# Weight residuals by accumulating transfers, and Hyena transforms modulo 4 in float32, in a two-layer hybrid encoder

## The chip, the cores and the metric

The kernel runs on one core of one Trainium2 chip. The metric is the device time of one execution in microseconds (us), the median of several runs. TensorE multiplies matrices, VectorE, ScalarE and GpSimd do elementwise work, and SyncE issues transfers. The profile calls them PE (with PEld for its weight loads), DVE, ACT, POOL and SP.

## The reference

The model has two layers over 512 tokens of 1024 channels, all in float32:

```
h = RMSNorm(x);  p = h @ W_in                # 1024 x 2176
A: 384 channels, bidirectional RG-LRU with a convolution and a GeLU gate
B: 6 query heads, 2 key heads, attention within 128 tokens, with a sink logit
C: 256 channels, Hyena: y = irfft(rfft(z, 1024) * rfft(filter, 1024)) + z * bias, times a gate
x = x + concat(RMSNorm(A), RMSNorm(B), RMSNorm(C)) @ W_out      # 1024 x 1024
x = x + relu(RMSNorm(x) @ W_up)^2 @ W_down                      # 1024 x 4096, 4096 x 1024
```

After both layers comes one final RMSNorm.

## The kernel before, in words

**Products in three terms.** Float32 products are made from float32r operands. `split` and, for weights, `split_weight` round a value to a hi part (a cast) and keep the rest as a lo part (a subtraction). `mm3` issues three matmuls: hi by hi, hi by lo and lo by hi. So every weight tile of 128 by 1024 words (512 KB) costs a load, a cast on ACT or DVE, and a subtraction on DVE or POOL (`nc.any`).

**Weight tiles.** In both layers together there are 34 tiles of W_in (the first loaded in two halves), 16 of W_out, 64 of W_up, and 64 loads of W_down, which are combined into seven products for each of 16 quads (a Strassen-Winograd scheme, `PRODUCTS`), so 112 tiles. An in or an up tile feeds 24 matmuls of 512 columns. `weight` emits a tile `LA` tiles ahead of its use; `load` makes a tile's load wait for the end of an earlier tile's preparation. Raw words, hi parts and lo parts have pools of 6, 3 and 3 tiles.

**Order.** All instructions are first recorded and then ordered by `Plan.schedule`, a list scheduler with prices for each instruction. It decides at build time which engine takes an instruction that more than one could do. Work is given out in the order of recording, save where `plan.prio` is set. `SCRIPTS` sets the order of the steps in a layer's mixer: a number is an in tile, `G` the gates of the RG-LRU, `R` and `U` attention, `F` the Hyena filters, `I` the loading of what comes later, `H` the Hyena convolution, `S` and `A` the scans and the output of the RG-LRU, `N.` a group norm and `O.` an out projection. Where TensorE would sit idle, the planner puts in small bf16 matmuls whose results nobody reads (tile `wk`, in `filler`).

**Hyena.** The transform of length 1024 uses cosine and sine tables at odd frequencies. The sequence is split into even and odd positions (`dft`, called for `He`, `Ho`, `Xe`, `Xo`); the six tables, the filters, the inputs and the spectra `G` are each split into hi and lo, and each product is three matmuls of 256 columns. The inverse (tile `y`) does the same.

**End.** The last stage treats tokens in two halves. It scales `x` by the reciprocal norm, transposes it (tile `fin`), scales by the gain while leaving PSUM, and stores 16 pieces of 128 KB.

Of the kernel before, what the change touches and what calls it, by code (L numbers as in the profile page):

```python
# [10 lines left out]
F32 = mybir.dt.float32  # L11
# [19 lines left out]
    "8 10 F 1 9 3 0 G0 2 11 12 G2 G1 7 6 R 5 16 U U 15 U I 4 U S 13 U U 14 H U U NB A NA OA NC OB OC",  # L31
    "16 1 G1 6 2 0 15 G2 14 G0 11 13 12 7 H 9 8 10 R U 5 U 4 U U U U U 3 NC S U OC A NA OA NB OB",
)]
LA = 2
# [135 lines left out]
class Plan:  # L170
# [112 lines left out]
    def schedule(self):  # L283
# [31 lines left out]
        while pending:  # L315
            moved = True
            while moved:
                moved = False
                for e in engines:
# [76 lines left out]
                    if o.dma:  # L396
                        dma_free = max(dma_free, t + 1.0) + c
                        free_at[e] = t + 0.45
                        end = dma_free + 1.2
                    else:  # L400
                        end = t + c
                        free_at[e] = end
                    if LOCK and (e == "gpsimd" or e == "vector" and self.two_port(o)):
                        port_free = end
# [55 lines left out]
def encoder_kernel(ctx, tc, xT, w_in, w_out, w_up, w_down, gates, fw, par, trig, rope, decay, zemb, ident_d, maskb_d, yT):  # L460
# [81 lines left out]
    def split_weight(raw, n, c, hi, lo):  # L542
        plan.either(
            ("scalar", "copy", dict(out=hi[:, :n], in_=raw[:, :n])),
            ("vector", "tensor_copy", dict(out=hi[:, :n], in_=raw[:, :n])),
        )
        nc.any.tensor_tensor(out=lo[:, :n], in0=raw[:, :n], in1=hi[:, :n].bitcast(F32), op=ALU.subtract)
        return [(hi[:, q * c:q * c + c], lo[:, q * c:q * c + c]) for q in range(n // c)]

    def wtile(pool_, dt, name):  # L550
        return pool_.tile([128, 1024], dt, name=name, tag=name)

    def load(raw, src):
        if len(wdone) >= 3:
            plan.extra = {wdone[-3]}
# [32 lines left out]
    def emit_weight(key):  # L588
# [10 lines left out]
        else:  # L599
# [5 lines left out]
            out = split_weight(raw, 1024, 128 if kind in ("in", "up") else 512, wtile(whi, F32R, "wh"), wtile(wlo, F32R, "wl"))  # L605
# [128 lines left out]
    def load_trig(which):  # L734
        tr = {}
        for n in which:
            raw = Fs("traw")
            nc.sync.dma_start(out=raw, in_=trig[n])
            tr[n] = split(raw, "trig")
# [15 lines left out]
    def dft(tabs, src, out):  # L755

        th, tl = [t.rearrange("p (c k) -> p c k", c=2) for t in tabs]
        sh, sl = [t.rearrange("p (c k) -> p c k", c=2) for t in src]
        for kt in range(2):
            o = out[:, kt * 256:(kt + 1) * 256]  # L760
            for c in range(2):
                ks = slice(kt * 128, kt * 128 + 128)
                mm3(o, th[:, c, ks], tl[:, c, ks], sh[:, c, :], sl[:, c, :], c == 0, c == 1)

    def filters(i, tr):
# [15 lines left out]
        for par_ in range(2):  # L781
# [14 lines left out]
            hs.append(split(s, "hs"))  # L796
            hd.append(split(d, "hd"))
        H = {}
        for nm, tb, src in (("c", (0, 4), hs), ("s", (1, 5), hd)):
            pe = PMX("He")  # L800
            dft(tr[tb[0]], src[0], pe)
            e = Fs("e")
            nc.scalar.copy(out=e, in_=pe)
            po = PMX("Ho")
            dft(tr[tb[1]], src[1], po)
            for sg, op in (("+", ALU.add), ("-", ALU.subtract)):
                H[nm + sg] = Fs("H" + nm + ("p" if sg == "+" else "m"))
                nc.vector.tensor_tensor(out=H[nm + sg], in0=e, in1=po, op=op)
        return H

# [27 lines left out]
    nc.any.tensor_scalar(out=hbias, in0=pcols(_cols["ba"][0], _cols["bx"][1]), scalar1=0.5, scalar2=1.0, op0=ALU.mult, op1=ALU.mult)  # L838
    nc.any.tensor_scalar(out=nsink, in0=pcols(*_cols["sink"]), scalar1=-1.0, scalar2=1.0, op0=ALU.mult, op1=ALU.mult)
    nc.any.tensor_scalar(out=s_, in0=lam, scalar1=-1.0, scalar2=1.0, op0=ALU.mult, op1=ALU.mult)  # L840
    nc.vector.tensor_tensor(out=ex, in0=lam, in1=s_, op=ALU.min)
    act(ex, ex, AF.Exp)
    nc.any.tensor_scalar(out=s2, in0=ex, scalar1=2.0, scalar2=1.0, op0=ALU.add, op1=ALU.mult)
    nc.vector.reciprocal(out=s2, in_=s2)
    nc.any.tensor_tensor(out=s_, in0=ex, in1=s2, op=ALU.mult)
    nc.any.tensor_tensor(out=s2, in0=s_, in1=s_, op=ALU.mult)
    nc.any.memset(pl, 2.0 / 17.0)
    for q in range(7, -1, -1):
        nc.any.tensor_tensor(out=pl, in0=pl, in1=s2, op=ALU.mult)
        nc.any.tensor_scalar(out=pl, in0=pl, scalar1=2.0 / (2 * q + 1), scalar2=1.0, op0=ALU.add, op1=ALU.mult)  # L850
    nc.any.tensor_tensor(out=pl, in0=pl, in1=s_, op=ALU.mult)
    nc.vector.tensor_scalar(out=s_, in0=lam, scalar1=-1.0, scalar2=0.0, op0=ALU.mult, op1=ALU.max)
    nc.any.tensor_tensor(out=pl, in0=pl, in1=s_, op=ALU.add)
    nc.any.tensor_scalar(out=m4sp, in0=pl, scalar1=-4.0, scalar2=1.0, op0=ALU.mult, op1=ALU.mult)
    nc.any.tensor_scalar(out=p4sp, in0=pl, scalar1=4.0, scalar2=1.0, op0=ALU.mult, op1=ALU.mult)
# [8 lines left out]
    for i in range(DEPTH):  # L864
# [254 lines left out]
        def hyena(H, tr):  # L1119
# [5 lines left out]
            for par_ in range(2):  # L1125
                p = PMX("zt")
                for c in range(2):
                    for n in range(2):
                        src = v[n].rearrange("p (c s two) -> p c two s", c=2, two=2)[:, c, par_, :]
                        nc.tensor.transpose(p[:, c * 256 + n * 128:c * 256 + n * 128 + 128], src, ident)  # L1130
                zt.append(split(p, "zt"))
            X = {}
            for nm, tb in (("c", (0, 4)), ("s", (1, 5))):
                pe = PMX("Xe")
                dft(tr[tb[0]], zt[0], pe)
                e = Fs("e")
                nc.scalar.copy(out=e, in_=pe)
                po = PMX("Xo")
                dft(tr[tb[1]], zt[1], po)
                for sg, op in (("+", ALU.add), ("-", ALU.subtract)):  # L1140
                    X[nm + sg] = Fs("X")
                    nc.vector.tensor_tensor(out=X[nm + sg], in0=e, in1=po, op=op)
# [11 lines left out]
            for nm in "cs":  # L1154
                for pr, op in ((0, ALU.add), (1, ALU.subtract)):
                    g = Fs("G")
                    nc.any.tensor_tensor(out=g, in0=Y[nm + "+"], in1=Y[nm + "-"], op=op)
                    G[nm, pr] = split(g, "G")
            out = []
            for n in range(2):  # L1160
                p = PMX("y")
                for pr in range(2):
                    o = p[:, pr * 256:(pr + 1) * 256]
                    q = 0
                    for nm, tb in (("c", (2, 4)), ("s", (3, 5))):
                        th, tl = [t.rearrange("p (c k) -> p c k", c=2) for t in tr[tb[pr]]]
                        gh, gl = [t.rearrange("p (c k) -> p c k", c=2) for t in G[nm, pr]]
                        for c in range(2):
                            ch = slice(n * 128, n * 128 + 128)
                            mm3(o, gh[:, c, ch], gl[:, c, ch], th[:, c, :], tl[:, c, :], q == 0, q == 3)  # L1170
                            q += 1
# [5 lines left out]
                yv = y.rearrange("p (s two) -> p two s", two=2)  # L1177
                pv = p.rearrange("p (two s) -> p two s", two=2)
# [7 lines left out]
        for step in SCRIPTS[i]:  # L1186
            if step.isdigit():
                in_tile(int(step))
            elif step[0] == "G":
                lru_gates(int(step[1]))  # L1190
# [271 lines left out]
```

## Time and profile before

| | |
|---|---|
| median of 3 runs | 1106.83 us (1106.38 to 1107.84) |
| time of the profiled execution | 1107.12 us |
| its span (first to last instruction) | 1105.3 us |
| PE busy | 1090.6 us, 99% |
| DVE busy | 896.6 us, 81% |
| ACT busy | 588.6 us, 53% |
| POOL busy | 245.1 us, 22% |
| mean share of the transfer engines | 28.9% for the loads and stores |

Busy time of PE is the union of its instructions, and the ends of matmuls are modelled, so it doesn't tell how fast a matmul follows the one before. The start-to-start distance in the timeline, or the count in a stretch, does. Fillers count as busy.

### The profile page before, as it was taken

What the parts mean: (1) busy time and instruction counts of PE and PEld (TensorE: products, weight loads), DVE (VectorE), ACT (ScalarE), POOL (GpSimd) and SP (SyncE); (2) the same over time, 40 slices, a digit from 0 to 9 for tenths busy, and PEclk for the clock granted to TensorE, in tenths of its full rate; (3) what the DMA queues carried; (4) which work ended last, traced back from release to release, by engine and by line L of the source; (5) the groups of instructions that cost most, each with busy time, mean ns of one, the idle gap of its engine ahead of it and who ended that gap; (6) DMA issues with size and microseconds to landing.
All of it is one profiled execution on the core that took longest, in us unless ns stands there. A gap on an engine that the chain in (4) does not pass through costs nothing. (4 is left out here: it accounts for less than half of the span.)

```text
span 1105.3 us, 14023 instructions
## 1 busy us (share of the span) xinstructions
PE 1090.6 (99%) x5186; PEld 886.0 (80%) x5186; DVE 896.6 (81%) x1363; ACT 588.6 (53%) x957; POOL 245.1 (22%) x149
## 2 busy tenths in 40 slices
PE   9999999999999999999999999999999999999997
PEld 6778778888887788888887877788888888888886
DVE  8999988658779886797989999675597797788796
ACT  6677863455445454344366737745555445445444
POOL 0233443301011040110333234342011011011032
PEclk9999999999999999999999999999999999999999
DMA  9514101212243322422352221022141341342312
GB/s 341 189 52 156 67 32 54 100 59 94 77 146 103 109 90 83 134 76 77 104 173 78 79 74 58 20 74 92 64 130 46 129 134 59 114 133 70 102 58 77
DMA packets 35132, 107.90 MB, mean 98 GB/s; under 512 B 4150, under 2 KB 6710, under 8 KB 35064
## 3 DMA queue, kind: packets, MB, share of 16 engines
q1 hardware_dynamic: 35064, 107.01, 28.9%
q8 instruction: 41, 0.67, 0.3%
q14 instruction: 27, 0.22, 0.1%
HBM read 104.90 MB, written 2.10 MB: 97 GB/s over the span
## 5 line engine op out<-in xcount | busy, mean ns | idle before, releaser
L456 ACT CAST wh<-wr 128x1024 fp32r<-128x1024 f32 x197 | 207.4, 1054 | 346.4 <-PE pu L456 133.8
L456 DVE TENSOR_TENSOR wl<-wr,wh 128x1024 fp32r<-128x1024 f32 (+1 forms) x167 | 208.8, 1253 | 132.2 <-ACT wh L456 128.2
L456 PE MATMUL pu<-xgh,wh 128*128 128x512 f32 x512 | 199.4, 389 | 0.0
L456 PE MATMUL pu<-xgh,wl 128*128 128x512 f32 x512 | 199.4, 390 | 0.0
L456 PE MATMUL pu<-xgl,wh 128*128 128x512 f32 x512 | 199.3, 389 | 0.0
L456 POOL TENSOR_TENSOR wl<-wr,wh 128x1024 fp32r<-128x1024 f32 x60 | 146.2, 2439 | 228.2 <-ACT wh L456 174.7
L456 PEld LDWEIGHTS pu<-xgh,wl 128*128 128x128 f32 x512 | 96.1, 188 | 21.4 <-issue 1.6
L456 PEld LDWEIGHTS pu<-xgh,wh 128*128 128x128 f32 x512 | 96.1, 188 | 20.1 <-ACT xgh L456 0.2
L456 PEld LDWEIGHTS pu<-xgl,wh 128*128 128x128 f32 x512 | 96.1, 188 | 19.7
L456 PE MATMUL pin<-xgh,wh 128*128 128x512 f32 x272 | 107.7, 396 | 0.9 <-DVE p L456 0.4
L456 PE MATMUL pin<-xgh,wl 128*128 128x512 f32 x272 | 107.5, 395 | 0.0
L456 PE MATMUL pin<-xgl,wh 128*128 128x512 f32 x272 | 107.2, 394 | 0.3 <-DVE xgl L456 0.3
L456 POOL TENSOR_TENSOR s<-s,h 128x256 f32<-128x256 f32 x12 | 8.9, 742 | 397.4 <-ACT wh L456 388.5
L456 DVE TENSOR_TENSOR wr<-wr 128x1024 f32<-128x1024 f32 x61 | 72.8, 1219 | 0.0
L456 PEld LDWEIGHTS pin<-xgl,wh 128*128 128x128 f32 x272 | 51.1, 188 | 13.4 <-DVE xgl L456 2.1
L456 PEld LDWEIGHTS pin<-xgh,wh 128*128 128x128 f32 x272 | 51.1, 188 | 12.3 <-DVE p L456 0.8
L456 PEld LDWEIGHTS pin<-xgh,wl 128*128 128x128 f32 x272 | 51.2, 188 | 10.4 <-issue 0.2
L456 DVE SCALAR_TENSOR_TENSOR x<-po,tr,x 128x512 f32<-128x512 f32 x48 | 35.0, 747 | 23.2 <-PE po L456 19.8
L456 PE MATMUL po<-wh,ygh 128*128 128x512 f32 x128 | 50.6, 395 | 0.0
L456 PE MATMUL po<-wl,ygh 128*128 128x512 f32 x128 | 50.2, 392 | 0.0
L456 PE MATMUL po<-wh,ygl 128*128 128x512 f32 x128 | 50.0, 393 | 0.0
L456 DVE SCALAR_TENSOR_TENSOR x<-pY,r,x 128x512 f32<-128x512 f32 x64 | 45.6, 745 | 4.9 <-PE pY L456 4.9
(312 smaller groups left out, 2353.8 us busy)
## 6 DMA issues: line engine op xcount, KB each, us to landing
wr<-in_w_up SPq DMA_DIRECT2D x64, 512.0 KB, 3.4
wr<-in_w_down SPq DMA_DIRECT2D x64, 512.0 KB, 4.3
wr<-in_w_in SPq DMA_DIRECT2D x33, 512.0 KB, 4.0
wr<-in_w_out SPq DMA_DIRECT2D x16, 512.0 KB, 3.5
x<-in_xT SPq DMA_DIRECT2D x16, 256.0 KB, 5.6
dec<-in_decay SPq DMA_DIRECT2D x8, 256.0 KB, 7.3
out_y<-fin SPq DMA_DIRECT2D x16, 128.0 KB, 1.9
traw<-in_trig SPq DMA_DIRECT2D x6, 256.0 KB, 6.4
```

Source lines behind the costliest of these rows:

```text
L456: getattr(getattr(nc, o.eng), o.name)(*[res(a) for a in o.args], **{k: res(v) for k, v in o.kw.items()})
```

## The change

1. **Lo parts by transfers.** For in, out and up tiles from the fifth weight on, the lo tile is first written as the negated raw words rounded to float32r, on ACT or DVE; a transfer issued on POOL's queue then adds the raw words onto it. Down tiles and the first four weights keep the subtraction.
2. **One weight pool** of 13 tiles for raw, hi and lo parts, instead of 6, 3 and 3; the pool of 2 KB tiles shrinks from 69 to 67. The lookahead grows from 2 to 3 tiles, and a load waits for the preparation of the fourth tile back instead of the third. The planner's prices know transfers issued by POOL.
3. **Hyena modulo 4.** Positions are split by their remainder modulo 4. There are four tables, of 128 frequencies, used in float32 with no split; `sums` multiplies, `spectrum` combines by additions and subtractions, and the inverse has a further stage `U` of sums before its matmuls.
4. **Last stage** token tile by token tile, with a matmul against a diagonal matrix of the reciprocal norms in the place of scaling and transposing, and 8 stores of 256 KB in rows of 512 bytes.
5. **Order.** New `SCRIPTS`; the parameters of the gates are computed ahead of the first gates instead of at the very start.

```diff
-LA = 2
+LA = 3
+AHEAD = 4
+BY_DMA = ("in", "out", "up")
+WT, WRES = 13, 2
...
-    wraw = pool("wraw", 6, reserve=6)
-    whi = pool("whi", 3, reserve=3)
-    wlo = pool("wlo", 3, reserve=3)
-    sp = pool("sp", 69, reserve=RESERVE)
+    wraw = whi = wlo = pool("wt", WT, reserve=WRES)
+    sp = pool("sp", 67, reserve=RESERVE)
...
-    def split_weight(raw, n, c, hi, lo):
+    def split_weight(raw, n, c, hi, lo, by_dma=False):
...
-        nc.any.tensor_tensor(out=lo[:, :n], in0=raw[:, :n], in1=hi[:, :n].bitcast(F32), op=ALU.subtract)
+        if by_dma:
+
+            plan.either(
+                ("scalar", "activation", dict(out=lo[:, :n], in_=raw[:, :n], func=AF.Copy, scale=-1.0)),
+                ("vector", "tensor_scalar", dict(out=lo[:, :n], in0=raw[:, :n], scalar1=-1.0, scalar2=None, op0=ALU.mult)),
+            )
+            nc.gpsimd.dma_start(out=lo[:, :n].bitcast(F32), in_=raw[:, :n], accum_op=ALU.add)
+        else:
+            nc.any.tensor_tensor(out=lo[:, :n], in0=raw[:, :n], in1=hi[:, :n].bitcast(F32), op=ALU.subtract)
...
-        if len(wdone) >= 3:
-            plan.extra = {wdone[-3]}
+        if len(wdone) >= AHEAD:
+            plan.extra = {wdone[-AHEAD]}
...
+    def sums(tab, par, src, name):
+
+        p, b = PMX(name), Fs("b")
+        for c in range(2):
+            q, h = par + 2 * c, slice(c * 256, c * 256 + 256)
+            nc.tensor.matmul(out=p[:, h], lhsT=tab[:, q * 128:q * 128 + 128], rhs=src[:, h], start=True, stop=True)
+        nc.scalar.copy(out=b[:, :256], in_=p[:, 256:512])
+        return p[:, :256], b[:, :256]
+
+    def spectrum(tr, even, odd, name):
...
+        for nm, tab in (("c", 0), ("s", 1)):
+            a, b = sums(tr[tab], 0, even[tab], name + "e")
+            comb(e[nm][:, lo], a, b, ALU.add)
+            comb(e[nm][:, hi], *((a, b) if nm == "c" else (b, a)), ALU.subtract)
+        for nm, tab in (("c", 0), ("s", 1)):
+            for n in range(2 if odd[0] is not odd[1] else 1):
+                src = odd[tab] if n == 0 else odd[1 - tab]
+                a, b = sums(tr[tab], 1, src, name + "o")
...
+                for q in range(4):
+                    o = p[:, q * 128:q * 128 + 128]
+                    c = (q // 2) * 256 + n * 128
+                    for k, nm in enumerate("cs"):
+                        nc.tensor.matmul(out=o, lhsT=U[nm, q % 2][:, c:c + 128], rhs=tr[2 + k][:, q * 128:q * 128 + 128], start=k == 0, stop=k == 1)
...
+    for t in range(4):
         plan.prio = -0.5
...
+        r = token_rstd((t,))
+        d = Fs("diag")
+        nc.vector.tensor_scalar(out=d[:, :128], in0=ident, scalar1=r[:, 0:1], scalar2=1.0, op0=ALU.mult, op1=ALU.mult)
+        for n in range(2):
+            p, y = PMX("fin"), Fs("fin")
+            y.parts = True
+            for k in range(4):
+                c = slice(k * 128, k * 128 + 128)
+                nc.tensor.matmul(out=p[:, c], lhsT=x[t][n][:, c], rhs=d[:, :128], start=True, stop=True)
```

## Rows read from the trace of the kernel before

**Rows 1.** Page, part 1: busy time, share of the span and instructions.

```profile
PE 1090.6 (99%) x5186; PEld 886.0 (80%) x5186; DVE 896.6 (81%) x1363; ACT 588.6 (53%) x957; POOL 245.1 (22%) x149
```

**Rows 2.** Windows: busy us and instructions by engine, granted clock, transfers.

```profile
10.00:16.00 6.00, 6.00 (x29) 3.67 (x27) 6.00 (x16) 6.00 (x10) 0.00 (x0) 1.00 1.04 399
...
600.00:700.00 100.00, 96.78 (x518) 77.24 (x517) 96.12 (x159) 64.24 (x128) 35.73 (x23) 1.00 0.19 64
...
800.00:1085.00 285.00, 285.00 (x1262) 235.45 (x1261) 231.80 (x309) 136.01 (x181) 44.96 (x24) 1.00 0.29 95
```

**Rows 3.** Waits of PE: total us, times, longest.

```profile
PE vt L456 <- DVE p L456: 1.6, 1, 1.6
```

**Rows 4.** Windows of the filler's tile alone: PE busy us (instructions).

```profile
0.00:16.00 16.00, 7.12 (x42) 1.00 0.89 309
...
1090.00:1105.40 15.40, 3.72 (x31) 0.95 0.40 137
sum 1105.40, PE 21.48; mean PE 2.39
```

**Rows 5.** Groups by form on PE: the Hyena matmuls.

```profile
L456 PE MATMUL y<-trigh,Gh 128*128 128x256 f32 x32 | 8.9, 285 | 0.4 <-ACT Gh L456 0.4
...
L456 PE MATMUL Xo<-zth,trigh 128*128 128x256 f32 x16 | 4.6, 289 | 0.7 <-DVE rq L456 0.7
...
L456 PE MATMUL He<-hsl,trigh 128*128 128x256 f32 x8 | 2.3, 287 | 0.0
```

**Rows 6.** Timeline of PE: a run of Hyena matmuls, first and next after.

```profile
62.53 0.32 PE L456 MATMUL He<-hsl,trigh 128*128 128x256 f32 x1
...
68.20 0.40 PE L456 MATMUL pin<-xgh,wh 128*128 128x512 f32 x1
```

**Rows 7.** Timeline of PE: matmuls with float32 operands and what follows.

```profile
26.22 1.02 PE L456 MATMUL ssq<-sq,ones 128*128 128x512 f32 x2
27.17 1.07 PE L456 MATMUL f<-zemb,fw 33*64 33x512 f32 x2
...
54.97 3.70 PE L456 MATMUL f<-fw,h 64*128 64x512 f32 x8 [1.25 <-ACT h L456]
...
152.72 1.00 PE L456 MATMUL ssq<-ones,sq 128*128 128x1 f32 x8
153.58 0.38 PE L456 MATMUL wk<-warmc 128*128 128x256 bf16 x2
```

**Rows 8.** Groups by form: the preparation of weight tiles.

```profile
L456 DVE TENSOR_TENSOR wl<-wr,wh 128x1024 fp32r<-128x1024 f32 x165 | 207.4, 1260 | 132.2 <-ACT wh L456 128.2
...
L456 DVE CAST wh<-wr 128x1024 fp32r<-128x1024 f32 x28 | 19.2, 688 | 2.6 <-PE po L456 1.9 <-PE pu L456 0.7
...
L456 ACT CAST wh<-wr 128x1024 fp32r<-128x1024 f32 x197 | 207.4, 1054 | 346.4 <-PE pu L456 133.8 <-PE pY L456 82.0 <-PE pZ L456 45.0
...
L456 POOL TENSOR_TENSOR wl<-wr,wh 128x1024 fp32r<-128x1024 f32 x60 | 146.2, 2439 | 228.2 <-ACT wh L456 174.7 <-DVE wh L456 29.3 <-PE pin L456 14.0
```

**Rows 9.** Transfers: queue's packets, MB and share; issues, KB, us to landing.

```profile
q1 hardware_dynamic: 35064, 107.01, 28.9%
...
wr<-in_w_up SPq DMA_DIRECT2D x64, 512.0 KB, 3.4
wr<-in_w_down SPq DMA_DIRECT2D x64, 512.0 KB, 4.3
```

**Rows 10.** Timeline of the end, and the landing of the stores.

```profile
1091.40 0.75 DVE L456 SCALAR_TENSOR_TENSOR x<-pY,r,x 128x512 f32<-128x512 f32 x1 [0.34 <-PE pY L456]
...
1094.08 8.76 SPq L456 DMA_DIRECT2D out_y<-fin  x16
...
DMA to landing us min/median/max: 1.8/1.9/4.2
```

**Rows 11.** Timeline of DVE at the start.

```profile
12.51 0.17 DVE L456 TENSOR_SCALAR sp<-sp 128x12 f32<-128x12 f32 x1
12.58 0.74 DVE L456 SCALAR_TENSOR_TENSOR xgl<-x,pall,xgh 128x512 fp32r<-128x512 f32 x1
```

More of the change, by code (lines that the diff above doesn't have):

```diff
@@ L604, in emit_weight @@
                 load(raw, {"in": w_in, "up": w_up}[kind][i, key[2]] if kind != "out" else w_out[i, key[2]])
-            out = split_weight(raw, 1024, 128 if kind in ("in", "up") else 512, wtile(whi, F32R, "wh"), wtile(wlo, F32R, "wl"))
+            out = split_weight(raw, 1024, 128 if kind in ("in", "up") else 512, wtile(whi, F32R, "wh"), wtile(wlo, F32R, "wl"),
+                               kind in BY_DMA and wseq.index(key) >= 4)
         wdone.append(len(plan.ops) - 1)
@@ L736, in load_trig @@
         for n in which:
-            raw = Fs("traw")
-            nc.sync.dma_start(out=raw, in_=trig[n])
-            tr[n] = split(raw, "trig")
+            tr[n] = Fs("trig")
+            nc.sync.dma_start(out=tr[n], in_=trig[n])
         return tr
@@ L795, in filters @@
                 nc.any.tensor_tensor(out=d[:, cs], in0=f[:, 0:256], in1=f[:, 256:512], op=ALU.subtract)
[L796 to L809, printed above, removed]
+            hs.append(s)
+            hd.append(d)
+        return spectrum(tr, [hs[0], hd[0]], [hs[1], hd[1]], "H")
     def conv(i, u, taps, wname, bname, j, nj, centre):
@@ L837, in encoder_kernel @@
     hbias, nsink = ptile(12, "hbias"), ptile(6, "nsink")
[L838 to L850, printed above, removed]
@@ L1128, in hyena @@
                     for n in range(2):
-                        src = v[n].rearrange("p (c s two) -> p c two s", c=2, two=2)[:, c, par_, :]
+                        src = v[n].rearrange("p (r four) -> p four r", four=4)[:, par_ + 2 * c, :]
                         nc.tensor.transpose(p[:, c * 256 + n * 128:c * 256 + n * 128 + 128], src, ident)
[L1131 to L1142, printed above, removed]
+                z = Fs("zt")
+                rounded(z, p)
+                zt.append(z)
+            X = spectrum(tr, [zt[0], zt[0]], [zt[1], zt[1]], "X")
             Y = {}
@@ L1157, in hyena @@
                     nc.any.tensor_tensor(out=g, in0=Y[nm + "+"], in1=Y[nm + "-"], op=op)
-                    G[nm, pr] = split(g, "G")
+                    G[nm, pr] = g
+            U = {}
+            lo, hi = slice(0, 256), slice(256, 512)
+            for pr in range(2):
+                c, d = G["c", pr], G["s", pr]
+                U["c", pr], U["s", pr] = Fs("U"), Fs("U")
+                for nm, a, b in (("c", c, (c, d)[pr]), ("s", d, (d, c)[pr])):
+                    plus = nm == "c" or pr == 1
+                    nc.any.tensor_tensor(out=U[nm, pr][:, lo], in0=a[:, lo], in1=b[:, hi], op=ALU.add if plus else ALU.subtract)
+                    nc.any.tensor_tensor(out=U[nm, pr][:, hi], in0=a[:, lo], in1=b[:, hi], op=ALU.subtract if plus else ALU.add)
             out = []
@@ L1176, in hyena @@
                 )
-                yv = y.rearrange("p (s two) -> p two s", two=2)
-                pv = p.rearrange("p (two s) -> p two s", two=2)
+                yv = y.rearrange("p (r four) -> p four r", four=4)
+                pv = p.rearrange("p (four r) -> p four r", four=4)
                 nc.vector.scalar_tensor_tensor(out=yv, in0=pv, scalar=1.0 / 512.0, in1=yv, op0=ALU.mult, op1=ALU.add)
@@ L1189, in encoder_kernel @@
             elif step[0] == "G":
+                if i == 0 and not lru_st:
+                    gate_parameters()
                 lru_gates(int(step[1]))
```

109 lines of the change are left out of this document (55 added, 54 removed).

## The prediction

> **What bounds the kernel now.** I read the page's busy times first: PE is busy 99% of the span, DVE 81%, ACT 53%, POOL 22% [rows 1]. Since fillers count as busy, the second view is the windows. In the MLP of the second layer PE issues 1262 matmuls in 285 us, one every 0.226 us, and DVE is busy 232 of the 285 us [rows 2]. That is a pure PE bound: nothing but fewer or shorter matmuls makes this stretch shorter. From 600 to 700 us, the mixer of the second layer, DVE is busy 96% and PE's union falls to 96.8 us [rows 2]; there both engines are near their limit. At the start, from 10 to 16 us, DVE and ACT are busy all the time and the transfer engines' share is 1.04 [rows 2].
>
> Third come PE's waits: the longest of eleven is 1.6 us, for a value from DVE, and none is for a weight tile [rows 3]. The pauses long enough for fillers are in the windows of the filler's tile: of 21.5 us, 7.1 stand in the first 16 us and 3.7 in the last 15.4 [rows 4]. So there are three places to gain: the matmuls themselves, the start, and the end. Taking the subtractions of weights off DVE and POOL is worth little as long as no PE wait is for weights.
>
> **The Hyena matmuls.** Before there are 3 forms of `y` with 32, 6 of `X` with 16 and 12 of `H` with 8 matmuls: 96 + 96 + 96 = 288, all of 256 columns [rows 5]. A run of 47 of them goes from 62.53 to 68.20 us, so 0.1206 us each [rows 6], and all 288 take 34.7 us. After, by the diff, a layer has 6 calls of `sums` for the filters (even twice, odd four times, since the two sources differ) and 4 for the inputs, with 2 matmuls each: 20 of 256 columns. The inverse has 2 x 4 x 2 = 16 of 128 columns. Both layers: 40 and 32.
>
> These are float32 matmuls, and a float32 matmul leaves two records: the one sum over `ones` stands in the timeline as x2, 0.95 us from its start to the next matmul's, 0.475 us a record for 512 columns [rows 7]. The filters' matmuls give 3.70 / 8 = 0.46 [rows 7]. So there will be 80 records of 256 and 64 of 128 columns. No row has these widths in float32. In proportion to the columns they cost 0.228 and 0.114, together 18.2 + 7.3 = 25.5 us, a gain of 9.2; with 0.475 / 2 and 0.475 / 4 it is 26.6 and 8.1. That proportion is nearly right is seen in float32r: half the columns cost 0.1206 / 0.226 = 0.53 of the time. The upper end: with one column a record takes 0.86 / 8 = 0.1075 us [rows 7], and if that is a fixed part, a straight line through 0.1075 and 0.475 gives 0.291 and 0.199, in all 36.0 us, a loss of 1.3. I take 26.7 us, **a gain of 8 us**, since the 0.53 puts it near the proportional end; bounds +9.2 and -1.3. The gain counts in full where PE is the bound. The chain of combinations behind `sums`, and the new stage `U`, are hidden by the out products of the other groups and the rest of attention; without this cover each layer would show a few us of DVE work. DVE's own Hyena work hardly changes: in a layer ten subtractions for lo parts go, and 24 additions of half tiles come on top of the 8 of whole ones.
>
> **Lo parts by transfer.** 30 in, 16 out and 64 up tiles, 110 in all, lose a subtraction of 1.26 us on DVE or 2.44 on POOL and gain a negation, which I price like a cast: 1.05 on ACT or 0.69 on DVE [rows 8]. At most 110 x 1.26 = 139 us leave DVE. On PE's path this is worth nothing in the MLP, where PE waits for no weight. In the mixer, where DVE is near its limit, part of the short waits may go: **a gain of 2 us**, between 0 and 6 (eleven waits sum to about 8, all behind DVE, ACT or the start).
>
> The price is the transfer. No row shows one that adds, nor any issued from POOL; the only load queue is SP's [rows 9]. Below, it can cost what a load costs: 3.4 to 4.3 us to land [rows 9], and in engine time 28.9% of 1105 us for 107 MB, so 1.57 us for 0.524 MB. Above, with both operands read, twice that: 8.6 us and 3.1 us. The Trainium skill's page Collectives: The Full Stack (The bandwidth ceiling) says that an adding transfer costs double because it has two reads, not because of the addition; by that the upper figures would hold, and no run here shows it yet. Engine time is enough either way: a quad has 4 up and 4 down loads, and 4 additions at the upper price: 8 x 1.57 + 4 x 3.1 = 25 us, while PE works 4 x 24 + 7 x 12 = 180 matmuls, 40.7 us.
>
> Latency is covered too. With a lookahead of 3 tiles there are 3 x 24 x 0.226 = 16.3 us between one tile's turn and the preparation that must be ready. Load 4.3, cast 1.05, negation 1.05 and addition 8.6 make 15.0 us. So I cost the edit **at nothing**. What hides it is the lookahead; without it each tile would be late by the difference. Behind the POOL issue wait POOL's subtractions for down tiles (2.44 us each), whose own lookahead is 5. The wider shared pool lets this many tiles be open; should it not, loads start later, and the same cover shrinks.
>
> **Start.** Between the `xgl` subtractions DVE does one gate-parameter operation of 0.17 us each [rows 11]; moved away, and with two table loads fewer in the first rush and no table split, the first tiles may come **1 us** earlier. Bounds: 2, and minus 2, because the first additions join transfers whose share is already 1.04.
>
> **End.** Sixteen stores take SP 8.76 us, 0.55 each, the last issued at about 1102.8, while the last `x` is final at 1092.15 [rows 10]. After, 2 stores follow the last token tile in the place of 8: 6 x 0.55 = 3.3 us. ACT and DVE no longer scale `x`. Against this, rows of 512 bytes may land later, up to 4.2 instead of 1.9 us [rows 10], and the first two tiles' 32 records (at 0.114, 3.6 us), recorded at a priority ahead of the products, may stand before the last products. **A gain of 3 us**, between 0 and 5.
>
> **The sum:** 8 + 2 + 1 + 3 = 14 us. The profiled execution took 1107.1 us, 0.3 above the median of 1106.8, so the median becomes 1092.8; I say 1093.
>
> **Rivals.**
> 1. *Weights come late (slower).* The in tiles follow each other in both mixers. The period of a tile is its whole latency over three tiles of lookahead. It equals 5.43 us of PE work at 16.3 us, so at an addition of 16.3 - 6.4 = 9.9 us from POOL's turn to landing. Beyond it each us costs 0.33 us a tile; over all 94 in and up tiles 31 us, over the 30 in tiles alone 10. The gain of 14 is eaten at 0.45 us beyond if all suffer, at 1.4 if only the in tiles do. A chance for this comes from POOL's place in order: an addition can queue behind one or two subtractions of 2.44 us, and 8.6 + 2.44 passes 9.9 by 1.1. Both up and in tiles late by 1.14 give 1093 + 36 = 1129; in tiles alone 1104. Against it: at the lower price of 4.3 the cover has room for both subtractions.
> 2. *DVE holds up POOL's transfers (slower).* As a mechanism here: POOL can't make a transfer ready while a DVE cast runs, and each addition waits for one cast of 0.69 us [rows 8]. Alone that uses part of the cover; on top of rival 1 it makes 8.6 + 2.44 + 0.69 = 11.73, 1.83 beyond the cover, and 1093 + 57 = 1150. The Trainium skill's page SBUF — State Buffer (SBUF: two separate sides) states such a lock, between two-port copies on DVE and the descriptors of transfers issued from POOL. It gives 3.1 us for a transfer of 0.62 alone; by those 2.5 us more, the additions would land after 11.1 us, 1.2 beyond the cover, and the time would be 1131. The rule speaks against this change, and this trace has no transfer from POOL to show it.
> 3. *Savings turn into fillers (nearly no change to small gain).* If the mixers are bound by DVE from 600 to 700 us [rows 2] and in the first mixer likewise, shorter matmuls leave PE waiting, and only end and start remain: 1103. Against it: PE's listed waits are short, and DVE loses more work than it gains.
> 4. *More comes back.* DVE relief removes most of the waits and the start's fillers shrink by half (3.5 us): 8 + 6 + 3.5 + 5 = 22.5, so 1084.
>
> **How the numbers follow.** Forecast 0.60, rival 1 0.13, rival 2 0.05, rival 3 0.12, rival 4 0.10. The forecast's own range is 1087 to 1099 (its terms' bounds rarely fall together). With rival 4 below and rival 3 above, 0.82 lies between 1083 and 1104; less what the Hyena matmuls' upper price could push out, and with the mild part of rival 1 (in tiles alone, 1104 and some us), the range is 1083 to 1110. A change of 0.2%, 2.2 us, is about what a measurement of this kernel can tell from none. Faster: the forecast, rivals 3 and 4 without some mixed cases that end near no change, and a little of rival 1: 0.80. Same, from those mixed cases and the mildest of rival 1: 0.05. Slower, the rest of rivals 1 and 2: 0.15.
>
> **What would show it.** `He`, `Ho`, `Xe`, `Xo` with 256-column float32 records near 0.23 us apart, and 64 `y` records near 0.11; PE without waits for `wl`; additions landing under 9.9 us after POOL's turn; the last store issued within 8 us of the last `x`; DVE busy below 850 us. Wrong: PE waiting for DMA of `wl`, more fillers in the mixers, or 128-column records near 0.2.

## The result and the profile after

The change makes the kernel slower: 1115.08 us median of 18 runs against 1106.9 us of the kernel before in the same runs, ratio 1.0055 (95% interval 1.0042 to 1.0068). The forecast was 1093. The profiled execution took 1115.37 us, its span is 1113.5.

The page of the kernel after, part 1 and two queues of part 3 (packets, MB, share of 16 engines):

```profile
PE 1094.0 (98%) x5081; PEld 880.1 (79%) x5081; DVE 886.5 (80%) x1447; ACT 586.8 (53%) x957; POOL 211.3 (19%) x205
...
q0 software_dynamic: 15840, 57.68, 28.3%
q1 hardware_dynamic: 36696, 106.49, 26.7%
```

Against [rows 1] PE has 105 matmul records fewer, and DVE lost only 10 us, not the up to 139 that the 110 subtractions are worth. The windows of [rows 2]:

```profile
10.00:16.00 6.00, 5.91 (x27) 3.80 (x27) 6.00 (x10) 6.00 (x11) 0.00 (x0) 1.00 1.05 403
600.00:700.00 100.00, 96.94 (x508) 76.76 (x508) 91.22 (x171) 62.34 (x123) 21.93 (x22) 1.00 0.55 132
800.00:1085.00 285.00, 285.00 (x1271) 233.13 (x1270) 234.97 (x326) 124.38 (x165) 30.63 (x30) 1.00 0.51 142
```

The start is as before, the share of the transfer engines rises from 0.19 to 0.55 in the mixer and from 0.29 to 0.51 in the MLP, and DVE does as much in the MLP as before. There DVE has 51 subtractions instead of 62, but also all 24 negations of up tiles (16.6 us), while POOL's subtractions went from 16 to 2: the planner filled the freed time with work that ACT (136 to 124 us) and POOL (45 to 31) had. The windows of the filler's tile, cut by stage:

```profile
0.00:16.00 16.00, 7.21 (x41) 1.00 0.87 308
16.00:200.00 184.00, 0.49 (x3) 0.96 0.60 159
200.00:560.00 360.00, 4.53 (x32) 1.00 0.54 147
560.00:760.00 200.00, 5.67 (x40) 1.00 0.60 144
760.00:1090.00 330.00, 5.58 (x40) 1.00 0.52 142
```

From 16 to 200 us there are hardly any fillers, but the granted clock is 0.96. The waits of PE, to be held against [rows 3]:

```profile
PE pt L460 <- DVE e L460: 3.1, 1, 3.1
PE s L460 <- DVE kh L460: 2.0, 1, 2.0
PE fin L460 <- DVE ms L460: 1.4, 1, 1.4
```

The timeline of the kernel after, on several engines (start, us, operation, and in brackets the idle time ahead with its releaser). The new Hyena matmuls (`He`, `Ho`, `y`) are in it, and three places that cost time:

```profile
60.21 0.97 PE L460 MATMUL gate<-xch,gth 128*128 128x512 f32 x3 [1.24 <-ACT xch L460]
61.10 6.34 PE L460 MATMUL f<-fw,h 64*128 64x512 f32 x8
67.38 0.80 PE L460 MATMUL gate<-xcl,gth 128*128 128x512 f32 x1
...
72.93 1.02 PE L460 MATMUL He<-hd,trig 128*128 128x256 f32 x4
73.79 1.03 PE L460 MATMUL Ho<-hs,trig 128*128 128x256 f32 x4
74.65 1.89 PE L460 MATMUL Ho<-hd,trig 128*128 128x256 f32 x8
...
110.64 0.85 SPq L460 DMA_DIRECT2D trig<-in_trig  x2
111.54 7.14 SPq L460 DMA_DIRECT2D x<-in_xT  x8
119.74 7.24 SPq L460 DMA_DIRECT2D wr<-in_w_out  x3
128.96 0.69 DVE L460 CAST wh<-wr 128x1024 fp32r<-128x1024 f32 x1 [3.65 <-DMA wr<-in_w_out]
128.97 1.06 ACT L460 ACTIVATE wl<-wr 128x1024 fp32r<-128x1024 f32 x1 [3.10 <-DMA wr<-in_w_out]
129.97 0.45 PE L460 MATMUL pt<-ident,e 128*128 128x128 f32 x2 [3.11 <-DVE e L460]
...
193.21 2.84 PE L460 MATMUL y<-trig,U 128*128 128x128 f32 x24
195.81 0.48 PE L460 MATMUL po<-wh,ygh 128*128 128x512 f32 x1
...
938.98 1.22 DVE L460 TENSOR_TENSOR wl<-wr,wh 128x1024 fp32r<-128x1024 f32 x1
941.88 1.27 PE L460 MATMUL wk<-warmc 128*128 128x256 bf16 x10
942.25 0.75 DVE L460 SCALAR_TENSOR_TENSOR x<-pY,r,x 128x512 f32<-128x512 f32 x1
943.05 0.50 PE L460 MATMUL pY<-wh,sah 128*128 128x512 f32 x1
```

What to see there:

- *The matmuls.* Four records of `He` take 0.86 us, so 0.215 each; 24 of `y` take 2.60, 0.108 each. For 80 and 64 records that is 17.2 + 6.9 = 24 us in place of 34.7 [rows 5, 6].
- *The stall at 127 us.* In the attention of the first mixer PE waits for `e` on DVE. DVE stands at the cast of a W_out tile whose load SP issued at 119.74, behind the loads of tables and `x`, and which landed 9.1 us later; ACT stands at the negation of the same tile. Neither engine can pass it, so ready attention work waits for a weight whose own turn comes later.
- *The clock.* The eight `f` took 6.34 us, where before they took 3.70 [rows 7].
- *The MLP.* PE had nothing for 1.17 us at 941.88: the next product (P6, the fourth of the quad on PE here) goes into the bank `pY` that DVE's update of `x` at 942.25 frees, and DVE did four `wl` subtractions of 1.22 us, this one the last, from 933.69 on ahead of it.

The windows for the clock (the column after POOL is the granted clock):

```profile
60.00:70.00 10.00, 9.79 (x17) 4.78 (x18) 8.03 (x12) 4.31 (x7) 2.90 (x3) 0.60 0.39 92
70.00:80.00 10.00, 10.00 (x42) 8.30 (x42) 8.09 (x18) 8.22 (x17) 1.70 (x1) 0.89 0.14 27
...
130.00:140.00 10.00, 10.00 (x47) 7.16 (x48) 7.48 (x18) 7.71 (x16) 2.75 (x3) 0.83 0.28 57
```

At the lower level (1.2 GHz, 0.5) for (0.40 + 0.11 + 0.17) x 20 = 13.6 us, PE loses 6.8 us of work. The fall at 130 follows the stall of 3.1 us. The fall at 62 follows a wait of 1.24 us; but before, a wait of 1.25 us ahead of the same eight `f` brought none [rows 7]. In the trace of e8_end_alone (below), whose first mixer is written as in the kernel before, the clock did fall there: the eight `f` took 5.44 us after a wait of 1.23, at 0.80 from 50 to 60 us. So after this wait the clock falls in some executions and not in others, also at the old lookahead; what decides is open. The runs of this kernel lie between 1109.65 us (mean granted clock 0.998) and 1119.6 (0.993), those of the kernel before around 1107 us (0.999) or around 1111 (0.995).

Transfers (issues, KB, median us to landing), and the issue of the additions on POOL (ns, least, median, most):

```profile
wl<-wr POOLq DMA_DIRECT2D x110, 512.0 KB, 5.4
wr<-in_w_up SPq DMA_DIRECT2D x64, 512.0 KB, 4.5
wr<-in_w_down SPq DMA_DIRECT2D x64, 512.0 KB, 7.0
```

```profile
L460 POOL DMA_DIRECT2D wl<-wr x110: 850/862/1155, 20.4 to 1042.2; - x110
```

An addition lands after 5.4 us, between the bounds 4.3 and 8.6; the slowest of the 110 took 9.8. The loads land later than before [rows 9].

### The profile page after: what moved, and what is told of

Its sections match the earlier page's. It is cut to its first block, busy times and chain, and to the rows that moved or that the text cites. A ratio compares the mean times of both kernels' runs of the same rounds, so it can differ in the third digit from the quotient of the medians.

```text
span 1113.5 us, 14163 instructions
## 1 busy us (share of the span) xinstructions
PE 1094.0 (98%) x5081; PEld 880.1 (79%) x5081; DVE 886.5 (80%) x1447; ACT 586.8 (53%) x957; POOL 211.3 (19%) x205
## 3 DMA queue, kind: packets, MB, share of 16 engines
q0 software_dynamic: 15840, 57.68, 28.3%
q1 hardware_dynamic: 36696, 106.49, 26.7%
## 4 chain that ended last, share of the span: by engine, by line
PE 82%; DVE 8%; DMA 4%; ACT 3%; issue 2%; SPq 0%; POOL 0%; ACTq 0%; DVEq 0%; POOLq 0%
PE pu L460 31%; PE pY L460 16%; PE pZ L460 8%; PE pin L460 7%; PE po L460 7%; PE pX L460 4%; PE gate L460 1%; PE pv L460 1%; PE f L460 1%; PE pt L460 1%; DMA wr<-in_w_in 1%; DVE wl L460 1%; DVE tg L460 1%; DMA zemb<-in_zemb 1%; DMA wr<-in_w_out 1%
## 5 line engine op out<-in xcount | busy, mean ns | idle before, releaser
L460 ACT CAST wh<-wr 128x1024 fp32r<-128x1024 f32 x190 | 198.7, 1051 | 289.8 <-DMA wr<-in_w_up 88.8
L460 POOL DMA_DIRECT2D wl<-wr x110 | 96.3, 878 | 529.1 <-DVE wl L460 192.1
L460 DVE TENSOR_TENSOR wl<-wr,wh 128x1024 fp32r<-128x1024 f32 (+1 forms) x108 | 131.1, 1220 | 22.0 <-ACT wh L460 19.5
L460 PEld LDWEIGHTS pu<-xgh,wh 128*128 128x128 f32 x512 | 96.1, 188 | 20.9 <-issue 1.1
L460 DVE TENSOR_SCALAR wl<-wr 128x1024 fp32r<-128x1024 f32 x73 | 51.8, 710 | 28.4 <-DMA wr<-in_w_up 22.9
L460 ACT ACTIVATE relu<-pu 128x512 f32<-128x512 f32 x64 | 37.9, 592 | 39.9 <-PE pu L460 39.9
L460 DVE TENSOR_TENSOR s<-h 128x256 f32<-128x256 f32 x62 | 28.1, 454 | 34.5 <-ACT h L460 34.2
L460 DVE SCALAR_TENSOR_TENSOR x<-pZ,r,x 128x512 f32<-128x512 f32 x64 | 46.9, 747 | 8.5 <-PE pZ L460 8.4
```

Of the source, the lines that this page charges most:

```text
L460: getattr(getattr(nc, o.eng), o.name)(*[res(a) for a in o.args], **{k: res(v) for k, v in o.kw.items()})
```

## The experiments

Eighteen kernels ran. The table reads from each trace when PE starts the first up matmul (end of the first mixer), how long the first MLP, second mixer and second MLP take (to the last product of a layer, to the next layer's first up matmul, to the last product), all in us. Ratios are against the kernel before on the same chip; its median there was between 1107 and 1110, so kernels are compared by ratio. A row's stages are those of one execution, and time lost at the lower clock (half of what is spent at it) is in them: in mixer 1, 6.8 us of after, 5.1 of e6, f4 and g2, 3.4 of e7 and e8, 1.7 of e1, e2, f3, h4 and h6, none of the others; in mixer 2, 3.4 of e2 and h4, 1.7 of e8, f4, k1, k5 and l1.

| kernel | mixer 1 | MLP 1 | mixer 2 | MLP 2 | median | ratio (95%) |
|---|---|---|---|---|---|---|
| before | 218.0 | 344.2 | 201.4 | 327.4 | 1106.83 | |
| after | 221.1 | 343.8 | 200.4 | 332.9 | 1115.08 | 1.0055 (1.0042 to 1.0068) |
| e1_no_transfers | 227.0 | 345.1 | 203.3 | 331.9 | 1121.94 | 1.0118 (1.01 to 1.0136) |
| e2_no_transfers_old_pools | 224.4 | 339.1 | 207.4 | 327.4 | 1114.29 | 1.0046 (1.0029 to 1.0062) |
| e6_hyena_alone | 227.3 | 339.1 | 209.9 | 327.4 | 1116.02 | 1.0068 (1.0051 to 1.0084) |
| e8_end_alone | 220.4 | 344.1 | 202.7 | 327.4 | 1107.77 | 0.9997 (0.9985 to 1.001) |
| f1_before_one_product | 218.3 | 337.8 | 202.2 | 327.4 | 1101.01 | 0.9941 (0.9919 to 0.9964) |
| f4_hyena_without_U | 224.2 | 339.1 | 200.7 | 327.4 | 1104.36 | 0.9971 (0.9958 to 0.9984) |
| e7_update_first | 218.4 | 342.7 | 202.4 | 328.1 | 1109.18 | 1.0007 (0.9987 to 1.0027) |
| f3_inout_update_first | 217.4 | 340.9 | 197.5 | 327.5 | 1102.3 | 0.9954 (0.9935 to 0.9972) |
| h4_old_hyena | 225.7 | 339.9 | 206.2 | 329.0 | 1114.51 | 1.0052 (1.0033 to 1.0071) |
| h6_old_hyena_la2 | 223.6 | 339.4 | 201.8 | 329.0 | 1108.77 | 0.9997 (0.9983 to 1.001) |
| g5_la2 | 209.9 | 340.7 | 200.7 | 327.5 | 1096.13 | 0.9887 (0.9867 to 0.9908) |
| g2_in_only | 225.1 | 340.6 | 200.7 | 327.5 | 1109.97 | 1.0007 (0.9992 to 1.0023) |
| k2_la2 | 210.2 | 355.8 | 213.8 | 349.3 | 1146.26 | 1.0333 (1.0309 to 1.0358) |
| k1_no_update | 209.9 | 345.7 | 215.8 | 330.4 | 1118.3 | 1.0083 (1.0061 to 1.0105) |
| k5_up_too | 210.2 | 365.3 | 219.6 | 358.7 | 1170.46 | 1.0556 (1.0528 to 1.0584) |
| g3_before_update | 217.2 | 343.2 | 204.5 | 328.9 | 1110.49 | 1.0017 (1.0 to 1.0034) |
| l1_mixer_la2 | 210.6 | 343.8 | 215.3 | 333.6 | 1119.48 | 1.0096 (1.0073 to 1.0119) |
| l2_mixer_la2_update | 210.3 | 342.6 | 202.1 | 328.2 | 1100.0 | 0.9933 (0.9911 to 0.9955) |

**1. Transfers off, then pools and lookahead too, and the parts alone.** On the change:

```diff
e1:
-BY_DMA = ("in", "out", "up")
+BY_DMA = ()
e2, in addition:
-LA = 3
-AHEAD = 4
+LA = 2
+AHEAD = 3
-    wraw = whi = wlo = pool("wt", WT, reserve=WRES)
-    sp = pool("sp", 67, reserve=RESERVE)
+    wraw = pool("wraw", 6, reserve=6)
+    whi = pool("whi", 3, reserve=3)
+    wlo = pool("wlo", 3, reserve=3)
+    sp = pool("sp", 69, reserve=RESERVE)
```

> The changed kernel with all lo parts by subtraction again; shared pool, lookahead 3, Hyena modulo 4, last stage and order stay. Theory A (the adding transfers are the cost: they double the transfer work, loads land late, ACT and DVE stand in order behind a load, PE stops): the MLP of layer 2 goes back to a quad period of 40.8 us from 41.2 to 42.3, the clock stays near 1.0, time 1096 to 1101. Theory B (the shared pool and the longer lookahead bunch the preparation of down tiles ahead of the updates of x that PE waits for): the quads stay at 41.2 to 42.3, time 1104 to 1110. Theory C (the longer chain of the new Hyena and its place in the order starve PE in the mixers): mixers as in the changed kernel, 1108 or more.

> As the run without transfers, but also with the pools of 6, 3 and 3 tiles and the lookahead of 2 of before; Hyena modulo 4, last stage and new order stay. Theory A: within 2 us of the run without transfers, 1096 to 1101. Theory B: at least 5 us below it, about 1097 against 1104 to 1110. Theory C: still above 1105.

Without transfers the change is slower still, so they are not what costs. With the old pools and lookahead back, 7.6 us return: the MLPs are 10.5 us shorter, the mixers 1.5 longer together (e2 loses 3.4 us more there by the clock).

Then the kernel before with the new Hyena alone (`load_trig`, `sums` and `spectrum`, the stage `U`, the tables), and with the new last stage alone:

> The kernel before with the Hyena transforms modulo 4 alone, in the old order. Matmul work falls by 10 us by the records of the changed kernel (64 of 0.112 and 80 of 0.216 us against 288 of 0.1206). Theories A and B: 1097 to 1100. Theory C: 1105 or more, with PE waits in the mixers that were not there before.

> The kernel before with the new last stage alone. My forecast's term: 3 us shorter, 1104. The rival (the float32 matmuls of the first token tiles push the last products back by as much as the stores save): 1106 to 1108. In the changed kernel's trace the last product starts at 1098.2 and the span ends at 1113.5, 15.3 us, against 14.3 before, so this rival has the trace on its side.

The new Hyena alone costs 0.68%: each mixer grows by about 9 us (in mixer 1, 5.1 of them go with the clock). e2 has the new order and the new last stage besides, and comes to 1.0046: with no transfers, the order is worth 3 us at most in mixer 1 and, without the clock's part, some 6 in mixer 2. MLP 1 is 5 us shorter, but not by its filter matmuls. In the kernel before two quads had 2.04 us of fillers each ahead of P6, which are gone. The windows of the filler's tile by stage, the wait of PE, and its timeline at the inverse, in e6_hyena_alone:

```profile
16.00:234.00 218.00, 8.14 (x70) 0.98 0.28 99
234.00:573.00 339.00, 1.71 (x11) 1.00 0.31 105
573.00:784.00 211.00, 12.79 (x102) 1.00 0.19 65
```

```profile
PE y L456 <- DVE U L456: 2.5, 1, 2.5
```

```profile
183.71 5.52 PE L456 MATMUL wk<-warmc 128*128 128x256 bf16 x49
189.07 3.79 PE L456 MATMUL y<-trig,U 128*128 128x128 f32 x32
```

With the chain through `U`, PE has nothing ahead of `y`: the fillers of the mixers are 20.9 us, where the kernel before has 2.66 + 0.76. The chain is not all of it. DVE ends the eight `U` sums of mixer 1 at 185.7 us, 3.4 us before the first `y`, and the planner fixed the number of fillers at build time; what else held `y` is not shown. And the longest wait of PE in e6 is another, 3.9 us for `p` on DVE at 113 us, which f4 has too. The new last stage alone changes nothing.

**2. Is PE's time in the mixers worth anything?** In the kernel before, only hi by hi in the Hyena transforms; and e6_hyena_alone without `U`:

```diff
f1:
-                mm3(o, th[:, c, ks], tl[:, c, ks], sh[:, c, :], sl[:, c, :], c == 0, c == 1)
+                nc.tensor.matmul(out=o, lhsT=th[:, c, ks], rhs=sh[:, c, :], start=c == 0, stop=c == 1)
f4:
+            U = G
```

(The inverse in f1 likewise.)

> The kernel before, in whose Hyena transforms only the product of the hi parts is computed (192 of 288 matmuls left out, 23 us of TensorE time; all casts, subtractions and additions on the other engines stay). Theory M (in the mixers the elementwise work on DVE and its chains are the bound; PE time saved there turns into fillers and waits, and only what is saved in the MLP, where the filters of layer 2 run, is gained): about 4 us for the MLP and little more, 1101 to 1106, with holes in the mixers. Theory P (PE is the bound throughout, as the prediction had it, and the loss of the new Hyena has another cause): 1084 to 1088.

> The kernel before with Hyena modulo 4 alone, as in e6, but with the 16 additions of half tiles of the stage U left out in each layer's eight sums (G goes straight into the inverse matmuls; the matmuls are as many). Theory M: the wait of y for U in mixer 1 (5.4 us of fillers in e6) and in mixer 2 (2.6 us) shrink by the chain left out, about 3 us each, so 1109 to 1113 against 1116 of e6. Theory P: within 1 us of e6.

Where 23 us of matmuls are left out, both mixers stay as long as they were; 6.4 us of MLP 1 are the gain, 3.8 of them in the quad with the filter matmuls; the two long quads are gone here too. Leaving out the 16 half-tile additions (eight a layer) makes e6_hyena_alone 1.0% faster, some 11 us, more than the 3 to 7 expected, while eight of them took 2.77 us on DVE, so 5.5 for all. Without transfers the mixers end by chains, not by PE: the mechanism of rival 3.

**3. The order of the `x` update, and the up tiles.**

```diff
e7 (on the change):
+                    plan.prio = -1.5
                     nc.vector.scalar_tensor_tensor(out=x[k][n], in0=o, scalar=sc[:, k:k + 1], in1=x[k][n], op0=ALU.mult, op1=ALU.add)
+                    plan.prio = 0.0
f3, in addition:
-BY_DMA = ("in", "out", "up")
+BY_DMA = ("in", "out")
```

> The changed kernel with one priority altered: in the down products the update of x on DVE is recorded ahead of the preparation of weights. Theory B, kept for the MLP alone (the longer lookahead and the shared pool bunch four subtractions on DVE ahead of the update that frees the bank of the next product): the quads go from 41.2 to 42.3 back to 40.8 us, 4 to 6 us less in all at the same clock, 1109 to 1111. Rival (the weights themselves are late in the MLP): quads unchanged.

> As the run with the update first, and lo parts by transfers for in and out tiles alone; up tiles are subtracted again. If the transfers' worth lies in the mixers, where DVE is short of time, and their price in the MLP: quads at 40.8, mixers as in the changed kernel, 1106 to 1110. If the up tiles' transfers help too: 1112 or more.

With the update first every quad of the second MLP lasts 40.8 us again instead of 41.2 to 42.3: 4.8 us in MLP 2. Without the up tiles it gains 7 us more, 5 of them in mixer 2, where no up tile is used but which was planned anew; it is faster than the kernel before and below both expected ranges.

**4. Old Hyena beside the transfers, lookahead, in tiles alone.** h4 is f3 with the Hyena and `SCRIPTS` of before (and pools of 12 and 69, into which its tiles fit); h6 and g5 are h4 and f3 with `LA = 2` and `AHEAD = 3`; g2 is f3 with `BY_DMA = ("in",)`.

> The kernel before, plus the transfers for in and out tiles, plus the shared weight pool (12 tiles, 2 KB pool of 69), the lookahead of 3 tiles, the new last stage and the x update of the down products first: run f3_inout_update_first with the Hyena of before and the order of before. Theory M (the mixers end by DVE and its chains, and the new Hyena lengthens them though it shortens PE): the mixers come out below those of f3 (217 and 198 us), by 4 to 9 us each, MLP 1 longer by about 5 because the filters' matmuls are back, in all 1092 to 1101, faster than f3's 1102.3. Rival (with transfers the mixers are bound by PE, and the matmul saving is real there): the 10 us of matmuls come back, 1108 to 1113.

> Run h4_old_hyena with a lookahead of 2 tiles and a load waiting for the third preparation back, as before. Theory: two tiles of lookahead are 10.9 us, load 4.3, cast and negation 2.1 and addition 5.4 make 11.8, so each in tile would be late by about 1 us, and the mixers grow by 5 to 15 us in all against h4. Rival: the pool and not the lookahead decides when loads start, and the time is that of h4 within 3 us.

> Run f3_inout_update_first with a lookahead of 2 tiles and a load waiting for the third preparation back, as before. Theory (the late w_out load in mixer 1 stands in front of other casts, because it is asked for too early relative to its turn and behind loads of x and tables): with a shorter lookahead the cast is asked for later and the wait of 3.9 us there goes: 1098 to 1101. Rival: the in tiles become late by 1 us each, 1106 to 1112.

> Run f3_inout_update_first with transfers for the in tiles alone; the 16 out tiles are subtracted again. Theory (what the transfers give is DVE's relief in the mixers; the out tiles are in the mixers too): the mixers grow by 1 to 5 us together, 1103 to 1107. Rival (the late w_out load with its queue of negation and addition costs more than the subtractions): 1098 to 1101.

Theory M fell in its general form. Beside the transfers the old Hyena is about 1% slower: h4 against f3 8 to 9 us in each mixer, h6 against g5 13.7 us in mixer 1 and 1.1 in mixer 2. There the new Hyena does pay, though the old order of steps goes with the old Hyena in these two. And the lookahead of 2, which should have made in tiles late, is faster both times, by 6 us. Mixer 1 falls to 209.9 us. The windows of g5_la2 over the stretches where the clock had fallen:

```profile
60.00:70.00 10.00, 10.00 (x42) 7.35 (x41) 8.76 (x21) 9.46 (x16) 3.72 (x5) 1.00 0.56 105
...
120.00:130.00 10.00, 9.91 (x56) 7.12 (x53) 9.96 (x21) 9.71 (x20) 2.37 (x2) 1.00 0.18 59
```

No stall and a full clock. g2_in_only loses 7.7 us in mixer 1 against f3 (3.4 by the clock), more than the 1 to 5 expected of both mixers: transfers for the 16 out tiles are worth it.

**5. Which of the three carries the loss.** k2 is the change with `LA = 2`, `AHEAD = 3`; k1 is g5 without the two `plan.prio` lines; k5 is g5 with up tiles too; g3 is the kernel before with the two lines.

> The change with the lookahead of 2 tiles and the third preparation back, as before; transfers for in, out and up tiles, update order as in the change. If the lookahead of 3 carries the loss (it lets preparations stand on DVE ahead of work that PE waits for): 1105 to 1110, 5 to 10 below the change. If the lookahead is what hides the transfers, as the prediction had it (16.3 us covers 15.0): each in and up tile late, 1118 or more.

> The fast version (run g5_la2, 1096.1) with the x update of the down products in its old place. If the update behind subtractions is what lengthens the quads whatever the lookahead: quads of 41.2 to 42.2 instead of 40.8 us, 1101 to 1104. If it needed the lookahead of 3: 1095 to 1098.

> The fast version with transfers for the up tiles too. If up transfers cost by themselves (f3 against e7 was 7 us, most of it in mixer 2 and MLP 1): 1101 to 1105. If they cost only with the lookahead of 3: 1095 to 1098.

> The kernel before with only the x update of the down products first. In it two quads of MLP 1 last 43.0 us and have 2.04 us of fillers in front of the sixth product. If the late update is their cause: these go, 4 us, 1102 to 1104, so what the fast version gains by the order isn't the change's. If the fillers there have another cause: 1106 to 1108.

With up tiles by transfer, the lookahead of 2 costs 31 us and more, nearly all in MLPs and mixer 2; k5 lies far above both of its ranges. k5_up_too, the timeline of an up tile on POOL and PE, and a wait of PE:

```profile
310.57 1.89 POOL L460 DMA_DIRECT2D wl<-wr  x2
...
316.32 0.39 PE L460 MATMUL pu<-xgl,wh 128*128 128x512 f32 x1
316.55 3.23 PE L460 MATMUL wk<-warmc 128*128 128x256 bf16 x28
319.53 0.48 PE L460 MATMUL pu<-xgh,wl 128*128 128x512 f32 x1
```

```profile
PE pu L460 <- DMA wl<-wr: 2.7, 4, 0.9
```

PE does all that needs `wh` and then runs 28 fillers before the first matmul with `wl`. But the first of the two additions had landed at 316.0 us, before the first filler, and the second lands at 320.0, after that matmul started, so this tile's `wl` was there. In all nine such places of k5 the fillers end 1.4 us or more after the landing, and the waits for `wl` that the profile shows come to 2.7 us; k2 shows none, and the fillers of its MLPs stand ahead of P6 and of the first matmul of up tiles. So the planner, which prices these transfers and places the fillers at build time, expected weights late, as rival 1 did; how much of the 31 us is late weights and how much is its price was not taken apart (`LA` also sets the down tiles' lookahead, 4 instead of 5). With this planner 3 is needed for up tiles. Without the update's order k1 has quads of 41.2 us at a lookahead of 2 too, where e2, with the old pools, has 40.8; so the shared pool does part of it without the longer lookahead. But k1's loss of 22 us against g5 is mostly mixer 2 (+15). On the kernel before, the order alone takes the two long quads away and gains nothing in all: MLP 1 is 1 us shorter, mixer 2 is 3 longer.

**6. The lookahead by kind.** The whole change, with

```diff
-        if len(wdone) >= AHEAD:
-            plan.extra = {wdone[-AHEAD]}
+        ahead = AHEAD - (wseq[wnext[0]][0] in ("in", "out"))
+        if len(wdone) >= ahead:
+            plan.extra = {wdone[-ahead]}
-        la = LA if key[0] != "down" else LA + 2
+        la = {"in": LA - 1, "out": LA - 1, "up": LA, "down": LA + 2}[key[0]]
```

and in l2 the update first too.

> The whole change, with a lookahead of 2 tiles (and loads that wait for the third preparation back) for in and out tiles, 3 (and the fourth) for up tiles as in the change. If the long lookahead in the mixers and the stalls and clock falls that it brings carry the loss: mixer 1 at 210 instead of 221 us, quads as in the change, 1102 to 1107. If up tiles are late again as in k2_la2: 1120 or more. If the mixers vary with every new order and mixer 2 grows by what mixer 1 gains: 1110 to 1116.

> As l1_mixer_la2, with the x update first. If both parts are independent: l1 less 6, 1096 to 1101, and quads of 40.8 us. If the transfers of up tiles cost by themselves (7 us between f3 and e7): 1102 to 1106. Rival as in l1.

l1 does in mixer 1 what was expected (210.6 instead of 221.1) and gives it back in mixer 2, which was expected of the third case, though its 1119.5 lies above that case's range. l2 is faster than the kernel before by 0.67%. Mixer 2 of the two, windows of the out products alone (the first of each fence) and of the fillers alone (the second), l1 and then l2:

```profile
660.00:725.00 65.00, 8.06 (x32) 0.97 0.37 88
...
660.00:725.00 65.00, 21.24 (x166) 0.97 0.37 88
```

```profile
660.00:725.00 65.00, 19.24 (x80) 1.00 0.37 84
...
660.00:725.00 65.00, 9.33 (x78) 1.00 0.37 84
```

In both this stretch holds the attention. In l2 80 out matmuls run between its steps, in l1 only 32, and fillers stand in the gaps. This is no scatter: k1 and k2, which also have a lookahead of 2 for in and out tiles and the update in its old place, have the same 166 fillers in mixer 2 and last 215.8 and 213.8 us there, l1 215.3; with the update first, g5 and l2 have 200.7 and 202.1. So the gain by the shorter lookahead hangs on the order of the update. Which edge in the planner moves the out products is open; it was not tried. From kernel to kernel mixer 2 lies between 197.5 and 219.6 us, so other differences of whole kernels in it are not put down to one edit here.

## Why the prediction was wrong

The forecast was 14 us faster, and the profiled span is 8.2 us longer: mixer 1 by 3.1, MLP 2 by 5.5, the end by 0.9, less 0.4 in MLP 1 and 1.0 in mixer 2.

**The step that failed** is "So I cost the edit **at nothing**. What hides it is the lookahead". The cover held: PE waits for no `wl` in the kernel after. But the longer lookahead and the shared pool have a price, which had no term in the sum:

- In the mixers the lookahead costs 10.5 us in mixer 1 alone (after against l1; in the six kernels with new Hyena, transfers and a lookahead of 2 there it is 209.9 to 210.6, in the three with 3 tiles and transfers for in and out 217.4 to 221.1). In the kernel after the place is seen: a preparation that is asked for early stands at the head of DVE's and ACT's queues while its load waits on SP's, and attention waits behind it, 3.1 us; 6.8 us more go with the clock. That the lookahead moves both is shown by the six with 2: from 16 us to the end of mixer 1 the longest wait of PE is 0.4 us and the clock is full. The first fall can come without it, as e8 shows, so the 6.8 us are not its price alone. In whole time the shorter lookahead pays only with the update first: l1 is 0.4% slower than after, l2 0.7% faster than e7.
- In the MLP the two put subtractions on DVE ahead of the update which frees P6's bank: 4.8 us in MLP 2 and 1.1 in MLP 1 (e7 against after).

With both put right (l2) the change runs at 0.9933 of the kernel before, half of the gain that was forecast.

**Point by point.**

- *Hyena matmuls:* forecast 26.7 us, measured 24, so a gain of 10.6 instead of 8. But a second step failed here: "The gain counts in full where PE is the bound", with the chain "hidden by the out products". On its own the new Hyena costs 0.68%, and in f1, where 23 us of matmuls are left out, the mixers stay as they were: there PE is not the bound. With transfers and a lookahead of 2 mixer 1 is 8 us shorter than before, where half of the Hyena's 8 us, half of the transfers' 2 and the start's 1 were to give 6. What separates the two cases is mostly the transfers with their pool: from e2 to k2, with the same Hyena, order and lookahead, mixer 1 goes from 224.4 to 210.2 us, while the order is worth 3 us at most there. The transfers and the pool were not taken apart, and the Hyena of before with the new order did not run.
- *Lo parts:* the landing, 5.4 us, lies in the predicted range, and the slowest, 9.8, just under the 9.9 of rival 1. The additions cost (28.3 / 57.68) / (26.7 / 106.49) = 1.96 times the engine time of a load per MB. The Trainium skill's page Collectives: The Full Stack (The bandwidth ceiling) puts an adding transfer at two reads; the trace agrees. The relief of DVE is smaller than thought (886.5 us busy, not below 850), but the transfers are worth more than the 2 us forecast: from e1 to after it is 7 us, 6 of them in mixer 1.
- *Start:* 7.21 us of fillers instead of 7.1, no gain in place of 1 us.
- *End:* from the last product to the end of the span 15.3 instead of 14.4 us, no gain in place of 3, as e8 shows: `fin` runs as float32 in 64 records instead of 32, and PE waits 1.4 us for `ms`. The step that failed is that 2 stores follow the last token tile: all 8 follow it, and the last is issued 10.2 us after the last `x`, as before (10.3), not within 8.

**The rivals.** Rival 1 did not happen at a lookahead of 3. At 2 the times came out as it feared (k2, k5), but fillers that the planner placed stand where PE would have waited, so how late the weights were is not shown. Rival 2 was not seen: POOL's issue took 0.850 to 1.155 us with a median of 0.862, so none was held up for long. The Trainium skill's page SBUF — State Buffer (SBUF: two separate sides) describes the lock; 110 issues beside a DVE that is busy 80% of the time do not show it. Whether this kernel's casts are copies of the kind that the page means, no run shows. Rival 3's mechanism is what e6 and f1 show in kernels without transfers; its time, 1103, missed the price of the lookahead. With the update first, up tiles subtracted and a lookahead of 2 the parts give 1096.13 us, 1.13% under the kernel before, some 12 us. That this is near the forecast 14 is luck in part: it is another kernel than the one forecast, and its terms differ from those of the sum.

## What to carry to other kernels

A longer lookahead is not free on engines that work in order: a preparation issued early blocks whatever stands behind it when its load is late, so give each kind of tile the lookahead that its own latency needs, and look for what waits behind it. Give an operation that frees a buffer PE waits for its place by hand ahead of work that is merely early. Where a planner fills PE's pauses at build time, hold the end of the fillers against the moment when the operand was ready: fillers tell what the planner expected, not what happened. In a kernel whose planner reorders everything, compare stages rather than totals, and cost a shorter matmul only where something else stands ready to fill its place.

## What was not expected of the hardware

A 512 KB addition within SBUF lands in 5.4 us and takes POOL 0.88 us to issue, 96 us for 110. The loads of W_down took 7.0 us to land beside them instead of 4.3, in f3, with no up tile by transfer, 3.5, but in k2, with as many additions and a lookahead of 2, 4.5; so the additions alone don't make them late. Float32 matmuls cost in proportion to their columns down to 128 of them: 0.215 us a record for 256, 0.108 for 128. After PE's waits of 1.24 and 3.1 us the clock stood at the lower level for 13.6 us in all, while a wait of 1.25 us before brought no fall, and one of 1.23 us at the same place in e8 did.
